# One decoder block on one core: the order of the attention steps on TensorE, the factor transposes and spread, and the pooling maps

## The chip, the cores and the metric

The kernel runs on one core of a Trainium2 chip. The metric is the device time of one execution in microseconds (us). A core has TensorE (PE in the profile; its weight loads are shown apart as PEld), VectorE (DVE), ScalarE (ACT), GpSimd (POOL), and SyncE (SP), which here only issues transfers. Each engine works through its own list of instructions in order and waits at semaphores for the others.

## The reference, cut to what matters

One layer, 512 tokens, width 1024: a SwiGLU layer, a token-mixing layer, a second SwiGLU layer, and a final norm, all modulated by a condition vector. The change lies in the token mixing:

```python
def token_mixing(u, cos, sin, w_in, w_pool, pool_scale, w_pool_branch, w_attn_branch, w_out):
    proj = u @ w_in
    p, q, k, v, gate_logits = jnp.split(proj, cuts, axis=-1)
    y_pool = multiscale_pool(p, w_pool, pool_scale)      # per group g: trailing mean minus token, times w_pool[g] (64x64), times scale
    q, k = rope(q), rope(k)
    for gi, (window, dilation) in enumerate(((128, 1), (512, 4), (2048, 16))):   # 4 heads of 64 each
        o, lse = dilated_window_attention(q[gi], k[gi], v[gi], window // dilation, dilation)
    wts = softmax(stack(lses))                           # over the three groups
    y_attn = sum_g wts[g] * outs[g]
    g_pool, g_attn = split(sigmoid(gate_logits))
    merged = g_pool * (y_pool @ w_pool_branch) + g_attn * (y_attn @ w_attn_branch)
    return merged @ w_out
```

## The kernel before, in words

Activations lie as channels by tokens: 128 channels on the partitions, 512 tokens along them, the tokens stored by residue class (c = token mod 4, then i = token div 4, "p (c i)"). All large products are made from two parts, high and low (`whi`, `wlo` of the weights, `UH`, `UL` of the activations): ScalarE writes the high part (line 377), VectorE subtracts to get the low part (line 389), and TensorE adds three products (lines 421 to 423 for 512 columns; 750 to 752 for 256 columns; 1779 to 1781 for the value tiles). The splits run a few tiles ahead of TensorE, in a ring. The order on every engine is the order in which the Python code issues the instructions; there is no scheduler.

The attention is cut into units (kind, n, hp): kind 0 is the undilated group (four blocks n of 128 queries), kind 1 are the two dilated groups together (four residue classes n = c); hp is a pair of heads. Each unit passes through five steps:

- `at_scores`: products of q and k, 64 rows deep (one head lies on 64 partitions), into `bS`; line 1470.
- `at_exp`: VectorE adds the mask and takes the maximum (1486, 1488), ScalarE the exponential (1491), which gives `prob`.
- `at_turn`: TensorE transposes `prob` in blocks of 128x128 into `bT` (1503), ScalarE copies to `probT` (1506, 1509).
- `at_values`: products of v (64 columns wide) and `probT` into `bO` (1521); for the second pair of heads VectorE copies `bO` out (1527 for kind 1, 1529 for kind 0).

These steps are strewn into the large products. `hooks` returns, for the sixth contraction step (k = 5) of a 512-column tile, a list of steps: the new units' scores, the transposes of the units whose scores were made one tile earlier, and the values of those of two tiles earlier. Eight projection tiles carry kind 0 (every second tile has new units, so transposes alternate with values and scores), the second pooling tile and the four value tiles (c = 0 to 3) carry kind 1. The last values of kind 1 are issued in the first gate product (`first`).

Then, inside the first group of gate products (`gate_duo`), `third` issues two things: `pool_map`, which multiplies the pooled differences `pd` (in `ev`, stored in token order "p (i c)") by the four 64x64 matrices of `wpool`, in four quarter tiles of the array (line 1622), and copies the two banks with the scale to a high part (ScalarE, 1626) and a low part (VectorE, 1627); and `at_fT`, which turns the eight softmax factors `f` of each 128-token block into eight rows over 512 tokens (line 1561), split into high rows 0 to 7 and low rows 32 to 39 of `fT` (1564, 1565). In the second group, `ends` calls `at_spread`: four products of `fT` with a 0/1 matrix `sel` (1571) that spread the factors to all channels, for `at_y` (1577 to 1579). `clear`, at the value tile c = 1, fills `fT` with zeros and writes `sel` (1760, 1761).

Of the kernel before, what the change touches and what calls it, by code (L numbers as in the profile page):

```python
# [9 lines left out]
F32R = mybir.dt.float32r  # L10
I32 = mybir.dt.int32
AF = mybir.ActivationFunctionType
OP = mybir.AluOpType

P = 128
T = 512
# [142 lines left out]
def chunk_widths():  # L159
    outs = [D] * (KT // 2 * (len(PARTS) - 1)) + [(FT - PARTS[-1][0]) * P] * KT  # L160
    f1 = [2 * FIRST * P] * KT + [D] * (2 * (FT - FIRST)), outs
    mix = [D] * 20 + [w for _, ms in GROUPS for w in [D] * 4 + [4 * P] * len(ms)] + [D] * KT
    return f1, mix, ([D] * (2 * FT), outs)


class Kernel:
# [5 lines left out]

    def plan(self):
        (i1, o1), mix, (i2, o2) = chunk_widths()
        self.chunks = []
        for name, ws in (("wf1i", i1), ("wf1o", o1), ("wmix", mix), ("wf2i", i2), ("wf2o", o2)):
            off, rec = 0, []
            for w in ws:
                rec.append((name, off, w))
                off += P * w  # L180
            self.chunks.append(rec)
# [1375 lines left out]
    def at_fT(self, bank):  # L1557

        nc, v = self.nc, self.nc.vector
        for n in range(4):  # L1560
            nc.tensor.matmul(bank[:8, n * P:n * P + P], self.f[:, n, :], self.ident, start=True, stop=True,
                             skip_group_check=True)
        by, b = (lambda x: x.rearrange("p (c n i) -> p n c i", c=4, n=4)), bank[:8].rearrange("p (n c i) -> p n c i", n=4, c=4)
        nc.scalar.activation(by(self.fT[:8]), b, AF.Copy)
        v.tensor_tensor(by(self.fT[32:40]), b, by(self.fT[:8]), op=OP.subtract)
# [48 lines left out]
    def pool_map(self, high, low):  # L1614

        nc = self.nc
        self.PH, self.PL = high, low
        banks = (self.bO, self.bS[0])
        for t in range(2):
            for r in range(2):  # L1620
                rows = slice(64 * r, 64 * r + 64)
                nc.tensor.matmul(banks[r][64 * t:64 * t + 64], self.wpool[rows, t * P + 64 * r:t * P + 64 * r + 64],
                                 self.pd[t][rows].rearrange("p (i c) -> p c i", c=4), start=True, stop=True, skip_group_check=True)
        for r, b in enumerate(banks):
            sc = self.vecs[:, 104 + r:105 + r]
            nc.scalar.activation(self.PH[r], b, AF.Copy, scale=sc)
            nc.vector.scalar_tensor_tensor(self.PL[r], b, sc, self.PH[r], op0=OP.mult, op1=OP.subtract)

    def mix(self):
        nc, tc = self.nc, self.tc  # L1630
# [8 lines left out]
        x = [xs[:, i * D:(i + 1) * D] for i in range(3)]  # L1639
# [4 lines left out]
        with tc.tile_pool(name="rt", bufs=1) as self.rt, tc.tile_pool(name="aw", bufs=2) as self.aw:  # L1644
# [5 lines left out]
            self.o23 = self.qt[0].rearrange("p (a t) -> p a t", a=2)  # L1650
            self.st, self.stn, self.f = (self.stp.tile([P, 4, 8], F32, name=x) for x in ("st", "stn", "f"))

            self.fT, self.sel = (self.stp.tile([64, T], F32R, name=x) for x in ("fT", "sel"))
            self.m1, self.l1 = (self.stp.tile([P, 16], F32, name=x) for x in ("m1", "l1"))
            masks = ma.tile([P, 4 * P], F32, name="masks")
            nc.sync.dma_start(masks, self.a["cst"][:, 163:675])
# [28 lines left out]
            for n in range(4):  # L1685
# [3 lines left out]
                b = self.nb()  # L1689
# [21 lines left out]

            def hooks(new, extra=(), between=()):
                sc, old = pipe
                todo = [(self.at_values, old), (self.at_turn, sc), (lambda f: f(), between), (self.at_scores, new),
                        (self.at_exp, new)]
                h = {5: [lambda f=f, u=u: f(u) for f, us in todo for u in us]}
                for k, f in extra:
                    h.setdefault(k, []).append(f)
                pipe[0], pipe[1] = list(new), sc
                return h  # L1720


            todo = [x for n in range(4) for x in ([(0, n, hp) for hp in range(2)], [])]
            rest = []
            for g in (1, 2):
                for dst in (self.qt[g], self.kt[g]):
                    for hp in range(2):
                        more = [((2, 7)[not hp], self.bg)] if dst is self.qt[1] else []
                        b = self.mm_tile(hooks(todo.pop(0), rest + more + [(7, self.bg)]))
                        rt = [self.scratch(2 * i + hp)[:, :T] for i in range(2)]  # L1730
                        self.rope_a(b, dst, hp, *rt)

                        rest = [(6, lambda dst=dst, hp=hp, w=rt[1]: self.rope_b(dst, hp, w))]


            g23 = [[(1, c, hp) for hp in range(2)] for c in range(4)]
            b = self.mm_tile(hooks([], rest + [(3, self.bg)]))
            self.pool_diff(0, b)
            assert self.ada_next == 59 and not self.adat, self.ada_next
# [11 lines left out]
            self.X, self.retired = [self.AR, self.cs], []  # L1751
            self.ready = True
            b = self.mm_tile(hooks(g23[0], [(3, u["copies"]), (4, u["adds"]), (7, self.bg)]))
            self.pool_diff(1, b)
            assert self.ada_next == 60 and not self.adat, self.ada_next
# [3 lines left out]
            def clear():  # L1759
                v.memset(self.fT.bitcast(F32), 0.0)  # L1760
                v.tensor_tensor(self.sel.rearrange("p (j d) -> p j d", j=8),
                                *(self.ident[:64, r:r + 8, None].to_broadcast([64, 8, 64]) for r in (0, 32)), op=OP.add)

            def free():
                self.held += 1
# [2 lines left out]

            held = self.held
            beside = [(1, 7, clear), (2, 2, lambda: u["whole"](0)), (2, 6, u["x0"]), (2, 6, u["x2"]), (2, 7, lambda: u["hi"](0)),  # L1770
                      (3, 0, u["x1"]), (3, 0, lambda: u["lo"](0)), (3, 2, self.at_swap), (3, 2, lambda: u["hi"](1)), (3, 3, free)]
            for c in range(4):
                hk = hooks(g23[c + 1] if c < 3 else [], [(k, f) for n, k, f in beside if n == c])
                b = self.nb()
# [436 lines left out]
```

## Time and profile before

| what | value |
|---|---|
| three runs | 966.43, 965.83, 966.37 us; median 966.37 |
| profiled execution: its own time | 965.6 us |
| its span (first to last instruction) | 963.7 us |
| granted TensorE clock | 0.999 |
| PE busy | 954.6 us (99%), 7278 matmuls |
| DVE, ACT, POOL busy | 839.2 us (87%), 539.4 us (56%), 88.5 us (9%) |

A busy time is the union of an engine's instructions. TensorE's instructions overlap in the pipeline (a 512-column product is shown as 0.39 us long, though the next one starts 0.23 us later), so the cost of a group on TensorE is read from start to start, not from its length. A plain fp32 product is shown as two records, a high and a low pass; the split products and the transposes as one.

### The profile page before, as it was taken

To read this page: it belongs to the slowest core of one execution; us is meant where nothing else is said; L and a number is where in the kernel's file an instruction comes from. 1 tells how busy PE (TensorE), PEld (TensorE's weight loads), DVE (VectorE), ACT (ScalarE), POOL (GpSimd) and SP (SyncE) were. 2 spreads that over 40 slices of the span, in tenths; PEclk is the share of its full clock that TensorE was granted. 3 is DMA by queue.
4 is the path that set the end of the run, shared out by engine and by line. 5 is a ranking of instruction groups with operands and counts; after the bars stand their busy time and mean duration, and the time that the engine had idled before them with its cause. 6 is when DMAs were issued, how large, how long until landed. Compare 5 with 4: busy or idle time off the path is not lost.

```text
span 963.7 us, 18130 instructions
## 1 busy us (share of the span) xinstructions
PE 954.6 (99%) x7278; PEld 897.1 (93%) x7278; DVE 839.2 (87%) x1237; ACT 539.4 (56%) x813; POOL 88.5 (9%) x106
## 2 busy tenths in 40 slices
PE   9999999999999999999999999999999999999997
PEld 7888999999999899878889998998999999999997
DVE  7989999899998779887897877989899888989886
ACT  5443666664755554444565453465665747566655
POOL 0000110101000003005410000000101100110002
PEclk9999999999999999999999999999999999999999
DMA  9857786786767648766356446724757666665632
GB/s 353 285 177 259 183 248 163 197 217 154 209 174 224 209 150 241 241 207 191 85 154 193 121 124 209 245 72 116 190 143 196 165 165 169 168 170 140 170 83 88
DMA packets 54087, 174.71 MB, mean 181 GB/s; under 512 B 7793, under 2 KB 10481, under 8 KB 53746
## 3 DMA queue, kind: packets, MB, share of 16 engines
q1 hardware_dynamic: 44416, 141.29, 44.6%
q0 software_dynamic: 9008, 31.72, 18.2%
q8 instruction: 57, 0.93, 0.4%
q10 hardware_dynamic: 578, 0.53, 0.2%
q14 instruction: 28, 0.23, 0.1%
HBM read 135.36 MB, written 2.24 MB: 143 GB/s over the span
## 4 chain that ended last, share of the span: by engine, by line
PE 92%; DVE 3%; DMA 2%; issue 1%; ACT 1%; POOL 0%; SPq 0%; POOLq 0%; DVEq 0%; ACTq 0%
PE bank L752 13%; PE bank L751 13%; PE bank L750 13%; PE bank L421 9%; PE bank L422 9%; PE bank L423 9%; PE bank L1111 4%; PE bank L1110 4%; PE bank L1109 4%; PE bank L2133 2%; PE bank L2135 2%; PE bank L2137 2%; DMA raw<-raw 1%; DVE wlo L389 1%; PE bank L1470 1%
## 5 line engine op out<-in xcount | busy, mean ns | idle before, releaser
L389 DVE TENSOR_TENSOR wlo<-raw,whi 128x1024 fp32r<-128x1024 f32 (+3 forms) x150 | 166.5, 1119 | 37.5 <-ACT whi L377 37.3
L750 PE MATMUL bank<-UH,whi 128*128 128x256 f32 x672 | 185.7, 276 | 0.0
L751 PE MATMUL bank<-UL,whi 128*128 128x256 f32 x672 | 185.6, 276 | 0.0
L752 PE MATMUL bank<-UH,wlo 128*128 128x256 f32 x672 | 185.6, 276 | 0.0
L389 DVE TENSOR_TENSOR wlo<-X,whi 128x1024 fp32r<-128x1024 f32 (+3 forms) x133 | 142.4, 1083 | 16.8 <-ACT whi L377 16.5
L377 ACT ACTIVATE whi<-raw 128x1024 fp32r<-128x1024 f32 (+3 forms) x150 | 142.6, 964 | 21.4 <-DMA raw<-wf1o 8.5
L377 ACT ACTIVATE whi<-X 128x1024 fp32r<-128x1024 f32 (+3 forms) x133 | 123.1, 946 | 52.8 <-DVE X L312 46.7
L750 PEld LDWEIGHTS bank<-UH,whi 128*128 128x128 f32 x672 | 126.1, 188 | 0.2
L751 PEld LDWEIGHTS bank<-UL,whi 128*128 128x128 f32 x672 | 126.3, 188 | 0.0
L752 PEld LDWEIGHTS bank<-UH,wlo 128*128 128x128 f32 x672 | 126.2, 188 | 0.0
L752 PE MATMUL bank<-SH,wlo 128*128 128x256 f32 x408 | 112.7, 276 | 0.3 <-DVE wlo L389 0.3
L750 PE MATMUL bank<-SH,whi 128*128 128x256 f32 x408 | 112.7, 276 | 0.0
L751 PE MATMUL bank<-SL,whi 128*128 128x256 f32 x408 | 112.6, 276 | 0.0
L421 PE MATMUL bank<-UH,whi 128*128 128x512 f32 (+1 forms) x272 | 92.8, 341 | 0.0
L422 PE MATMUL bank<-UL,whi 128*128 128x512 f32 (+1 forms) x272 | 91.9, 338 | 0.1
L423 PE MATMUL bank<-UH,wlo 128*128 128x512 f32 (+1 forms) x272 | 91.5, 337 | 0.0
L752 PEld LDWEIGHTS bank<-SH,wlo 128*128 128x128 f32 x408 | 76.6, 188 | 0.5 <-DVE wlo L389 0.5
L750 PEld LDWEIGHTS bank<-SH,whi 128*128 128x128 f32 x408 | 76.6, 188 | 0.1
L751 PEld LDWEIGHTS bank<-SL,whi 128*128 128x128 f32 x408 | 76.6, 188 | 0.0
L1109 PE MATMUL bank<-HI,whi 128*128 128x256 f32 x224 | 61.8, 276 | 0.0
L1110 PE MATMUL bank<-HK,whi 128*128 128x256 f32 x224 | 61.8, 276 | 0.0
L1111 PE MATMUL bank<-HI,wlo 128*128 128x256 f32 x224 | 61.8, 276 | 0.0
(408 smaller groups left out, 2404.3 us busy)
## 6 DMA issues: line engine op xcount, KB each, us to landing
raw<-wmix SPq DMA_DIRECT2D x44, 512.0 KB, 4.4
raw<-wf1i SPq DMA_DIRECT2D x32, 512.0 KB, 5.8
raw<-wf2i SPq DMA_DIRECT2D x30, 512.0 KB, 4.4
ada<-wada SPq DMA_DIRECT2D x23, 512.0 KB, 5.5
X<-raw POOLq DMA_DIRECT2D x23, 512.0 KB, 5.7
xs<-wada SPq DMA_DIRECT2D x17, 512.0 KB, 5.4
X<-wf2i SPq DMA_DIRECT2D x14, 512.0 KB, 4.5
X<-wf1i SPq DMA_DIRECT2D x11, 512.0 KB, 4.6
```

What stands on the lines that cost most here:

```text
L377: self.nc.scalar.activation(self.hi[:, y], r[:, x], AF.Copy)
L389: self.nc.vector.tensor_tensor(self.lo[:, y], r[:, x], self.hi[:, y], op=OP.subtract)
L421: M(ps, hi, uh, start=start, stop=False)
L422: M(ps, hi, ul, start=False, stop=False)
L423: M(ps, lo, uh, start=False, stop=stop)
L750: M(o, hi, uh, start=start and p == 0 and k == 0, stop=False, skip_group_check=True)
L751: M(o, hi, ul, start=False, stop=False, skip_group_check=True)
L752: M(o, lo, uh, start=False, stop=k == 3, skip_group_check=True)
L1109: M(o, hi, uh, start=start and m % 2 == 0 and k == 0, stop=False, skip_group_check=True)
L1110: M(o, hi, ul, start=False, stop=False, skip_group_check=True)
L1111: M(o, lo, uh, start=False, stop=k == 1, skip_group_check=True)
L2133: M(b, hi, self.UH[k], start=k == 0, stop=False)
```

## The change

Four edits:

1. In `hooks` the order of the steps at k = 5 becomes scores, values, transposes; it was values, transposes, scores. (`between` is never used.) The maximum and the exponential stay last.
2. `at_fT` uses the transpose operation in place of a product with the identity matrix.
3. `fT` and `sel` get 128 rows in place of 64 (the new ones hold zeros), so that the four spread products are 128 rows deep.
4. `pool_map` reads `pd` in the order in which it is stored; the result lies in the banks in token order, and the scaled copies of ScalarE and VectorE read the banks with a stride of four elements to write the residue-class order.

```diff
 def at_fT(self, bank):
-            nc.tensor.matmul(bank[:8, n * P:n * P + P], self.f[:, n, :], self.ident, start=True, stop=True,
-                             skip_group_check=True)
+            nc.tensor.transpose(bank[:8, n * P:n * P + P], self.f[:, n, :], self.ident)
...
 def pool_map(self, high, low):
-                                 self.pd[t][rows].rearrange("p (i c) -> p c i", c=4), start=True, stop=True, skip_group_check=True)
+                                 self.pd[t][rows], start=True, stop=True, skip_group_check=True)
         for r, b in enumerate(banks):
-            sc = self.vecs[:, 104 + r:105 + r]
-            nc.scalar.activation(self.PH[r], b, AF.Copy, scale=sc)
-            nc.vector.scalar_tensor_tensor(self.PL[r], b, sc, self.PH[r], op0=OP.mult, op1=OP.subtract)
+            sc, b = self.vecs[:, 104 + r:105 + r], b.rearrange("p (i c) -> p c i", c=4)
+            H, L = (x[r].rearrange("p (c i) -> p c i", c=4) for x in (self.PH, self.PL))
+            nc.scalar.activation(H, b, AF.Copy, scale=sc)
+            nc.vector.scalar_tensor_tensor(L, b, sc, H, op0=OP.mult, op1=OP.subtract)
...
-            self.fT, self.sel = (self.stp.tile([64, T], F32R, name=x) for x in ("fT", "sel"))
+            self.fT, self.sel = (self.stp.tile([P, T], F32R, name=x) for x in ("fT", "sel"))
...
             def hooks(new, extra=(), between=()):
-                todo = [(self.at_values, old), (self.at_turn, sc), (lambda f: f(), between), (self.at_scores, new),
+                todo = [(lambda f: f(), between), (self.at_scores, new), (self.at_values, old), (self.at_turn, sc),
                         (self.at_exp, new)]
...
             def clear():
-                                *(self.ident[:64, r:r + 8, None].to_broadcast([64, 8, 64]) for r in (0, 32)), op=OP.add)
+                                *(self.ident[:, r:r + 8, None].to_broadcast([P, 8, 64]) for r in (0, 32)), op=OP.add)
```

No instruction is added or taken away on any engine, and the lists of VectorE, ScalarE, GpSimd and SyncE keep their order; only TensorE's order changes, at six hooks. One of them is the hook of the value tile c = 1. On TensorE, between two products of that tile (lines 1781 and 1779; `bank_91` is its bank), there stood before:

```order
L1781 MATMUL bank_91<-whi,UL 128x512
L1521 MATMUL bank_97<-probT,v_3520 64x128 x8
L1503 MATMUL bank_90<-cst,prob 128x128 x4
L1503 MATMUL bank_92<-cst,prob 128x128 x4
L1470 MATMUL bank_93<-k_3517,q_3514 128x128
L1470 MATMUL bank_94<-k_3517,q_3514 128x128
L1470 MATMUL bank_93<-k_3518,q_3515 128x128
L1470 MATMUL bank_94<-k_3518,q_3515 128x128
```

and the last four rows once more, for the other pair of heads. Now, with the first four score rows above left out, there stand:

```order
L1470 MATMUL bank_93<-k_3517,q_3514 128x128
L1470 MATMUL bank_94<-k_3517,q_3514 128x128
L1470 MATMUL bank_93<-k_3518,q_3515 128x128
L1470 MATMUL bank_94<-k_3518,q_3515 128x128
L1521 MATMUL bank_97<-probT,v_3520 64x128 x8
L1503 MATMUL bank_90<-cst,prob 128x128 x4
L1503 MATMUL bank_92<-cst,prob 128x128 x4
L1779 MATMUL bank_91<-whi,UH 128x512
```

The scores moved from the end to the front, so the transposes (full tiles of the array) now stand next to the large products (full tiles too). At c = 2 it is the same; at c = 0 there are no values, and the transposes and the scores change places.

At three hooks of kind 0 there are values and scores and no transposes; the piece of the difference on TensorE at the second of them (bank_96 is the projection tile's bank):

```order
 L422 MATMUL bank_96<-UL,whi 128x512
 L423 MATMUL bank_96<-UH,wlo 128x512
-L1521 MATMUL bank_97<-probT,v_3519 64x128 x8
 L1470 MATMUL bank_93<-k_3516,q_3513 128x256
 L1470 MATMUL bank_94<-k_3516,q_3513 128x256
 L1470 MATMUL bank_93<-k_3516,q_3513 128x256
 L1470 MATMUL bank_94<-k_3516,q_3513 128x256
+L1521 MATMUL bank_97<-probT,v_3519 64x128 x8
 L421 MATMUL bank_96<-UH,whi 128x512
 L422 MATMUL bank_96<-UL,whi 128x512
```

Here the values moved behind the scores, and the number of neighbours of another kind stays the same.

## The prediction

> **What bounds the kernel now.** I read the page's busy times and its chain first, then the table of 20 us stretches, then TensorE's timeline at each place that the diff touches.
>
> ```profile
> PE 954.6 (99%) x7278; PEld 897.1 (93%) x7278; DVE 839.2 (87%) x1237; ACT 539.4 (56%) x813; POOL 88.5 (9%) x106
> PE 92%; DVE 3%; DMA 2%; issue 1%; ACT 1%; POOL 0%; SPq 0%; POOLq 0%; DVEq 0%; ACTq 0%
> 460.00:480.00 20.00, 20.00 (x149) 16.17 (x146) 16.82 (x35) 10.35 (x25) 8.98 (x7) 1.00 0.31 75
> ```
>
> TensorE is busy 99% of the span and carries 92% of the chain that ended last. In the stretch from 460 to 480 us it is busy all 20.00 us, at a granted clock of 1.00, while VectorE has 3.2 us free. So a microsecond taken from TensorE's list there is a microsecond of the program, as long as nothing that it waits for becomes late. The whole change is about TensorE's list, and the sum is made from start to start on it.
>
> **Part 1, the order of the steps.** TensorE pays when it passes from one shape of tile to another. The hook of the value tile c = 1, before:
>
> ```profile
> 458.96 0.39 PE L1781 MATMUL bank<-whi,UL 128*128 128x512 f32 x1
> 459.28 1.09 PE L1521 MATMUL bank<-probT,v 128*64 128x128 f32 x16
> 460.31 1.09 PE L1503 MATMUL bank<-cst,prob 128*128 128x128 f32 x8
> 461.33 1.16 PE L1470 MATMUL bank<-k,q 64*128 64x128 f32 x16
> 462.42 0.50 PE L1779 MATMUL bank<-whi,UH 128*128 128x512 f32 x1
> 462.76 0.40 PE L1780 MATMUL bank<-wlo,UH 128*128 128x512 f32 x1
> ```
>
> From the last product to the second one after the hook it takes 0.32 (into the values) + 1.03 (values) + 1.02 (transposes, then into the scores) + 1.09 (scores) + 0.34 = 3.80 us. How long the same stretches take beside other neighbours is shown at two other hooks. Transposes that are followed by a large product (c = 3):
>
> ```profile
> 478.04 1.10 PE L1503 MATMUL bank<-cst,prob 128*128 128x128 f32 x8
> 478.89 0.47 PE L1779 MATMUL bank<-whi,UH 128*128 128x512 f32 x1
> 479.20 0.40 PE L1780 MATMUL bank<-wlo,UH 128*128 128x512 f32 x1
> ```
>
> and scores that follow one and are followed by one:
>
> ```profile
> 383.68 0.39 PE L423 MATMUL bank<-UH,wlo 128*128 128x512 f32 x1
> 384.00 0.72 PE L1470 MATMUL bank<-k,q 64*128 64x128 f32 x8
> 384.64 0.50 PE L421 MATMUL bank<-UH,whi 128*128 128x512 f32 x1
> ```
>
> Eight transposes before a large product take 0.85 us, not 1.02; the step into scores costs 0.32, as that into values. The new order is 0.32 + 1.09 (scores) + 1.03 (values) + 0.85 (transposes) + 0.31 = 3.60 us: 0.20 saved, at c = 1 and at c = 2, 0.40 together. At c = 0 there are no values:
>
> ```profile
> 451.31 0.39 PE L1781 MATMUL bank<-whi,UL 128*128 128x512 f32 x1
> 451.54 1.04 PE L1503 MATMUL bank<-cst,prob 128*128 128x128 f32 x8
> 452.51 1.16 PE L1470 MATMUL bank<-k,q 64*128 64x128 f32 x16
> ```
>
> Before 0.23 + 0.97 + 1.09 + 0.34 (the last two as at c = 1) = 2.63; after 0.32 + 1.09 + 0.85 + 0.31 = 2.57; 0.06 saved. At the three hooks of kind 0 values and scores only change places. The values there, and the last ones of kind 1 before a large product:
>
> ```profile
> 409.94 1.09 PE L1521 MATMUL bank<-probT,v 128*64 128x128 f32 x16
> 410.97 1.14 PE L1470 MATMUL bank<-k,q 64*128 64x256 f32 x8
> ```
>
> ```profile
> 483.94 1.09 PE L1521 MATMUL bank<-probT,v 128*64 128x128 f32 x16
> 484.97 0.38 PE L427 MATMUL bank<-UH,whi 128*128 128x240 f32 x1
> ```
>
> Sixteen values take 1.03 us before scores and 1.03 before a large product, so nothing is won or lost there. What no row shows is the step from scores straight into values or transposes (six times now). I price it like the step from scores into a large product; the values before two different neighbours differ by 0.00, the transposes by 0.17, so between -0.05 and +0.05 at each is a fair bound: 0.3 us to either side. I take 0.46 us for part 1.
>
> Who waits differently: the copy of the values (1527, 1529) is ahead of the masked maximum in VectorE's queue, and the values come about 1.1 us later in the hook. At kind 0 VectorE reaches that copy late: in the hook above it starts at 412.86, and the values, which ended near 411.0, will end near 412.1. At c = 1 the new order is a gain:
>
> ```profile
> 412.86 0.42 DVE L1529 COPY o<-bank 128x256 f32<-128x256 f32 x1
> 462.52 0.42 DVE L1486 CUSTOM_DVE_ANT_0 prob<-bank,masks 128x256 f32<-128x256 f32 x1 [1.68 <-PE bank L1470]
> 476.18 0.69 DVE L1782 COPY v<-bank 128x512 f32<-128x512 f32 x1
> 477.01 1.09 PE L1521 MATMUL bank<-probT,v 128*64 128x128 f32 x16
> ```
>
> VectorE stood 1.68 us for the scores. Now they are there before the values, the copy runs when the values end near 461.4, and the maximum starts near 461.9, 0.6 us sooner. That matters, since VectorE then works without a wait up to the copy of `v` at 476.18, which ends (476.87) only 0.14 us before the values that read it. TensorE will be there 0.46 us sooner, VectorE 0.6: no stall.
>
> **Part 2, the factor transposes.** Parts 2 and 4 stand next to each other:
>
> ```profile
> 496.18 2.01 PE L1622 MATMUL bank<-ev,wpool 64*64 64x512 f32 x8
> 498.12 1.04 PE L1561 MATMUL bank<-cst,f 128*8 128x128 f32 x8
> 499.09 0.38 PE L427 MATMUL bank<-UH,whi 128*128 128x240 f32 x1
> ```
>
> The four products with the identity are eight records (two passes each) in 0.97 us. A transpose of `prob` is one record (eight of them in 0.85 us, 0.106 each), so four records go: 0.43 saved.
>
> The Trainium skill speaks against this term: TensorEngine Tiling (Array Packing), section Restrictions and Gotchas, says that column tiling excludes the transpose mode for fp32 input, and an output of eight rows is built into a tile of 32 columns. By that rule the two passes stay and the sum is smaller by 0.43; no row here has a transpose of so few columns.
>
> **Part 3, the spread.**
>
> ```profile
> 507.55 0.28 PE L751 MATMUL bank<-UL,whi 128*128 128x256 f32 x1
> 507.67 0.28 PE L752 MATMUL bank<-UH,wlo 128*128 128x256 f32 x1
> 507.88 1.20 PE L1571 MATMUL bank<-fT,sel 64*128 64x512 f32 x4
> 509.00 0.38 PE L427 MATMUL bank<-UH,whi 128*128 128x240 f32 x1
> 509.22 0.29 PE L750 MATMUL bank<-k,whi 128*128 128x256 f32 x1
> ```
>
> The step in costs 0.21 against 0.12 between equals, the four 512-column products 1.12 against 4 x 0.23 = 0.92 at the pace of the large ones (451.31 to 451.54), the step out 0.22 against about 0.12. At full depth all four are ordinary products: 0.09 + 0.20 + 0.10 = 0.39 saved, and never less than nothing, since the depth of a product does not lengthen it in these rows. The fill of `fT` and the write of `sel` on VectorE go over twice the partitions with as many elements on each; I cost them at nothing.
>
> **Part 4, the pooling maps.** The eight records (four quarter tiles at once, two passes) take 1.94 us, about 0.91 a pass, since the second four start at 497.1:
>
> ```profile
> L1622 PE MATMUL bank<-ev,wpool x8: 1074/1081/1092, 496.2 to 497.1; 64*64 64x512 f32 x8
> L1470 PE MATMUL bank<-k,q 64*128 64x256 f32 x24 | 3.4, 402 | 0.0
> ```
>
> For plain fp32 with operands in a row, eight score records of 128 columns take 0.64 us (384.00 to 384.64) and sixteen 1.09, so a pass of a pair costs 0.112 per 128 columns; 512 columns are 0.45. That is half of what the strided read takes. Bounds: nothing saved, if four streams at once are the limit, and 2 x (0.91 - 0.45) = 0.92. The values show two streams of 128 partitions at once, at (1.03 - 0.1) / 8 = 0.116 per pair and 128 columns; four streams of 64 partitions read as many rows, so I take the full 0.92.
>
> The Trainium skill has this in Advanced Engine Details and Errata, section Memory Cachelines: SBUF is read in lines of 16 bytes, and a read that finds each element in another line pays; four fp32 is just that stride. The length of 1081 ns agrees, and by that rule the 0.92 follows; without it the term would stay anywhere from 0 to 0.92.
>
> The stride now falls on two copies each of ScalarE and VectorE, out of the banks:
>
> ```profile
> L1626 ACT ACTIVATE xs<-bank,vecs 128x512 fp32r<-128x512 f32 x2 | 1.3, 686 | 0.0
> L1596 ACT ACTIVATE v<-bank 128x512 f32<-128x512 f32 x1 | 1.1, 1056 | 0.0
> 502.20 0.68 DVE L1565 TENSOR_TENSOR fT<-bank,fT 8x512 fp32r<-8x512 f32 x1
> ```
>
> A copy that writes with this stride takes 1056 ns, where one in a row takes 686; a strided read may cost nothing or as much. At the dear end ScalarE loses 2 x 0.4 and VectorE about as much. Behind them in the queues is `fT` (done at 502.88), which the spread reads at 507.88. That lead of 5.0 us shrinks by what TensorE saves before it (0.46 + 0.43 + 0.92 = 1.8) to 3.2, more than 1.6. So I cost it at nothing.
>
> **The sum.** 0.46 + 0.43 + 0.39 + 0.92 = 2.20 us less on TensorE. The profiled execution took 965.6 (span 963.7, 1.9 around it), so it would take 963.4; the median of the three runs is 0.8 above it, and on that median I predict 966.37 - 2.20 = 964.2. The later part follows, since ScalarE and VectorE there wait for TensorE again and again.
>
> **The rivals.** A measurement of this kernel tells 0.2% (1.93 us) from no change.
>
> - The pooling maps stay as long, because the four quarter tiles are the limit and not the stride. For it: no other row has four streams; against it: the two-stream pace. Gain 1.28, time 965.1. Chance 0.12.
> - The transposes of eight rows still take two passes. Gain 1.77, time 964.6. Chance 0.10.
> - A part of the gain turns into a wait: the copy of `v` with its 0.14 us of lead, if VectorE doesn't come sooner, holds TensorE by 0.46 - 0.14 = 0.32; with the unshown steps out of the scores dearer by 0.3 in all, the gain is about 1.6. Time 964.8. Against it: the 1.68 us that VectorE gets back. Chance 0.16.
> - Slower: the strided reads of the banks hold up `fT`. They decide once they add more than 3.2 us on ScalarE and VectorE in a row. At four times the length of 686 ns they add 2 x 2.06 = 4.1 on each, 8.2 together; the spread waits 5.0, less 2.2 won is 2.8 slower: 969.2. The nearest row shows 1.5 times, so chance 0.04.
> - The forecast: 964.2, chance 0.58, a little of which falls short of 0.2% since the sum is near that bound.
>
> **How the numbers follow.** Faster by over 0.2% (below 964.4): the forecast but for 0.04, and a step out of the scores that is cheaper than counted, 0.55 together. Within 0.2%: the first three rivals and that remainder, 0.41. Slower: 0.04. Low end: 0.3 more from the six unshown steps, 0.1 from a factor transpose that is a full tile and so saves its step out, and 0.4 for the spread of the runs: 963.4. High end: the pooling maps not shortened, and 0.2 lost beside it: 965.3. This leaves out the slow case and a few in a hundred at either end.
>
> **What would show it.** In the changed kernel's profile the hook at c = 1 should take 3.6 us from product to product, `prob` transposes should be followed by a large product 0.85 after their start, line 1561 should have four records, the pooling maps eight records of about 0.6 us within 1.0, the spread four records at a pace of 0.23 with no longer first one, and ScalarE's and VectorE's scaled copies their lengths under the stride. A wait of TensorE for the copy of `v` or for `fT`, eight records in line 1561, or pooling records still near 1.08 us would make the prediction wrong.

## The result and the profile after

The changed kernel took 963.2 us (median of 7, 962.49 to 964.25), the kernel before 966.37 on the same chip (median of 7, 965.83 to 968.3): ratio 0.9969, 95% interval 0.9959 to 0.9979. Measured again later, the ratio was 0.9966 (0.9954 to 0.9978). The kernel is faster. The forecast was 964.2 with a range of 963.4 to 965.3, so the sign was right and the time fell 0.2 us below the range: the gain was larger than the sum.

The busy times and the chain of the changed kernel's page (span 961.0 us, own time 962.81):

```profile
PE 952.0 (99%) x7274; PEld 896.5 (93%) x7274; DVE 838.4 (87%) x1237; ACT 539.1 (56%) x813; POOL 86.5 (9%) x106
PE 94%; DVE 2%; issue 1%; DMA 1%; ACT 1%; POOL 0%; POOLq 0%; ACTq 0%
```

TensorE is still the bound and has 2.6 us less of work, with four records fewer. The changed places follow in order of time. The hook of the value tile c = 1, TensorE's rows and then VectorE's:

```profile
458.41 0.39 PE L1781 MATMUL bank<-whi,UL 128*128 128x512 f32 x1
458.72 1.16 PE L1470 MATMUL bank<-k,q 64*128 64x128 f32 x16
459.82 1.09 PE L1521 MATMUL bank<-probT,v 128*64 128x128 f32 x16
460.84 1.09 PE L1503 MATMUL bank<-cst,prob 128*128 128x128 f32 x8
461.69 0.48 PE L1779 MATMUL bank<-whi,UH 128*128 128x512 f32 x1
462.01 0.40 PE L1780 MATMUL bank<-wlo,UH 128*128 128x512 f32 x1
```

```profile
460.96 0.43 DVE L1527 COPY q<-bank 128x256 f32<-128x256 f32 x1 [1.38 <-PE bank L1521]
461.54 0.42 DVE L1486 CUSTOM_DVE_ANT_0 prob<-bank,masks 128x256 f32<-128x256 f32 x1 [0.15 <-PE bank L1503]
474.94 0.68 DVE L1782 COPY v<-bank 128x512 f32<-128x512 f32 x1
```

From product to product it is 462.01 - 458.41 = 3.60 us, 0.20 less, as forecast; the transposes take 0.85 us up to the large product. VectorE reaches the maximum at 461.54 in place of 462.52 and the copy of `v` at 474.94 in place of 476.18; 0.48 of this the execution was ahead already at 446 us. The pooling maps and the factor transposes (L427 is an extra product of 240 columns that the kernel issues ahead of some gate products):

```profile
495.19 1.09 PE L1621 MATMUL bank<-ev,wpool 64*64 64x512 f32 x8
496.20 0.60 PE L1561 MATMUL bank<-cst,f 128*8 128x128 f32 x4
496.56 0.36 PE L427 MATMUL bank<-UH,whi 128*128 128x240 f32 x1
496.76 0.28 PE L750 MATMUL bank<-UH,whi 128*128 128x256 f32 x1
L1621 PE MATMUL bank<-ev,wpool x8: 589/614/640, 495.2 to 495.7; 64*64 64x512 f32 x8
```

Start to start, the pooling maps went from 1.94 to 1.01 us (records from 1081 to 614 ns), the factor transposes from 0.97 to 0.36, four records in place of eight. The strided copies out of the banks:

```profile
L1626 ACT ACTIVATE xs<-bank,vecs 128x512 fp32r<-128x512 f32 x2 | 1.3, 686 | 0.0
L1627 DVE SCALAR_TENSOR_TENSOR PL<-bank,vecs,xs 128x512 fp32r<-128x512 f32 x2 | 1.4, 744 | 0.0
```

ScalarE's take 686 ns as before, VectorE's 744 against 742: the stride costs nothing on this side. The spread:

```profile
504.83 0.28 PE L752 MATMUL bank<-UH,wlo 128*128 128x256 f32 x1
504.94 1.07 PE L1570 MATMUL bank<-fT,sel 128*128 128x512 f32 x4
505.85 0.27 PE L427 MATMUL bank<-UH,whi 128*128 128x240 f32 x1
505.96 0.28 PE L750 MATMUL bank<-k,whi 128*128 128x256 f32 x1
```

0.11 in, 0.91 for the four, 0.11 out, where it was 0.21, 1.12 and 0.22.

One thing had not been in any term. The gate products between the factor transposes and the spread were issued faster. Their groups in a stretch of 7 us, first before (500 to 507 us), then after (498 to 505); the last numbers are the busy time in us, the mean length of a record in ns, and the idle time ahead of them:

```profile
L751 PE MATMUL bank<-UL,whi 128*128 128x256 f32 x21 | 5.9, 281 | 0.0
...
L752 PE MATMUL bank<-UH,wlo 128*128 128x256 f32 x21 | 5.8, 276 | 0.0
```

281 ns go with one start every 117.8 ns, 276 with one every 113.3; no other values occur for long. The granted clock is 1.00 in both stretches. Some 65 of these products start 4.5 ns closer together, which is 0.28 us.

At 622 us a few tenths are given back. TensorE waits there for VectorE, which had itself waited for a load; the first row is that wait in the kernel before:

```profile
608.50 1.23 DVE L448 SCALAR_TENSOR_TENSOR v<-v,cond 128x1024 f32<-128x1024 f32 x1 [0.65 <-DMA v<-wada]
...
605.71 1.23 DVE L448 SCALAR_TENSOR_TENSOR v<-v,cond 128x1024 f32<-128x1024 f32 x1 [1.15 <-DMA v<-wada]
622.50 0.71 PE L509 MATMUL bank<-ones,AR 128*128 128x128 f32 x4 [0.21 <-DVE AR L624]
```

### The profile page after: what moved, and what is told of

It reads as the page before. It is cut to its first block, busy times and chain, and to the rows that moved or that the text cites. A ratio compares the mean times of both kernels' runs of the same rounds, so it can differ in the third digit from the quotient of the medians.

```text
span 961.0 us, 18119 instructions
## 1 busy us (share of the span) xinstructions
PE 952.0 (99%) x7274; PEld 896.5 (93%) x7274; DVE 838.4 (87%) x1237; ACT 539.1 (56%) x813; POOL 86.5 (9%) x106
## 4 chain that ended last, share of the span: by engine, by line
PE 94%; DVE 2%; issue 1%; DMA 1%; ACT 1%; POOL 0%; POOLq 0%; ACTq 0%
PE bank L750 14%; PE bank L752 14%; PE bank L751 14%; PE bank L421 8%; PE bank L422 8%; PE bank L423 8%; PE bank L1111 5%; PE bank L1109 5%; PE bank L1110 5%; PE bank L2133 2%; PE bank L2135 2%; PE bank L2137 2%; DMA v<-wada 1%; PE bank L1470 1%; PE bank L1521 1%
```

## How the runs are compared

Single executions of one kernel differ by a microsecond or more in places that the change doesn't touch. So each experiment is read locally: the ordinary products are the same in all kernels, and the start of each, less its start in the first profile of before, is a shift. The table (worked out from the traces, us, negative is earlier) gives by how much the shift changes in each stretch of before's time: 446 to 495 holds the steps of c = 0 to 3, 495 to 499.6 the pooling maps and factor transposes, 499.6 to 507.3 the gate products, 507.3 to 509.8 the spread, 509.8 to 560 what follows; "later" is 622 to 640, outside the sum.

```
kernel             446-495  495-499.6  499.6-507.3  507.3-509.8  509.8-560    sum   later
changed             -0.51     -1.55       -0.28        -0.44        0        -2.79   0.55
changed, again      -0.51     -1.55       -0.28        -0.44        0        -2.79   0.31
before, again        0.17      0           0            0           0         0.17  -0.01
order alone         -0.51      0           0            0           0        -0.51   0.39
transposes alone     0.01     -0.63        0           -0.01        0.62     -0.01   0.34
spread alone        -0.03      0           0           -0.40        0        -0.43   0.32
pool alone           0.01     -0.92       -0.29        -0.02        0        -1.21   0.28
changed, no settle  -0.51     -1.66       -0.29        -0.44        0        -2.90   1.33
changed, no settles -0.62     -1.66       -0.29        -0.56        0.62     -2.51   0.73
stride 2            -0.51     -1.50       -0.29        -0.44        0        -2.74   0.33
stride 8            -0.51     -0.60       -0.28        -0.44        0        -1.83   0.23
ft as 128x128       -0.51     -1.00        0           -0.42        0        -1.93   0.09
without pool        -0.51     -0.63        0           -0.41        0        -1.55   1.42
before, no settle    0.13     -0.11       -0.29        -0.02        0        -0.28   0.07
before, 224          0.16      0          -0.29        -0.02        0        -0.15   0.37
before, 256          0.18      0.01       -0.29        -0.02        0        -0.12   0.32
changed, 256        -0.51     -1.55       -0.29        -0.44        0        -2.79  -0.02
```

The changed kernel's stretch of 2.79 us comes back within 0.01 us in its second execution. All later readings use this table and the rows shown with them.

## The four parts, each alone

**The order** (line 1714 of before, nothing else):

```
-  todo = [(self.at_values, old), (self.at_turn, sc), (lambda f: f(), between), (self.at_scores, new),
+  todo = [(lambda f: f(), between), (self.at_scores, new), (self.at_values, old), (self.at_turn, sc),
```

> The kernel before, with the new order of an attention step alone (hooks and scores, then values, then transposes); transposes, spread and pooling maps as before. Theory A, that each part has its own price on TensorE and the prices add: the ordinary products of the changed kernel draw ahead of before's by 0.51 us between 446 and 484 us (0.06 in c=0, 0.20 in c=1, 0.20 in c=2, 0.03 in c=3), so here too 0.45 to 0.55 us, and nothing at the kind-0 steps; the pooling map stays at eight records of 1.08 us, the factor transposes at 0.97 us, the spread at 0.43 us more than after. Time 0.5 us under before if the loss near 625 us does not come, 0.0 to 0.2 if it does. Rival B, that the gain comes from the shorter wait of VectorE's maximum alone and is lost at the next wait on VectorE: the shift is back to under 0.2 us by 484.

965.91 us against 966.59, ratio 0.9994 (0.9984 to 1.0003): not told from before as a whole. Locally 0.51 us, at the same four places as in the changed kernel (0.08, 0.20, 0.20, 0.03), and nothing at the hooks of kind 0. Rival B falls: nothing is lost up to 560 us.

**The factor transposes** (line 1561):

```
-  nc.tensor.matmul(bank[:8, n * P:n * P + P], self.f[:, n, :], self.ident, start=True, stop=True, ...)
+  nc.tensor.transpose(bank[:8, n * P:n * P + P], self.f[:, n, :], self.ident)
```

> The kernel before, with the factor transposes as transposes (one pass) alone. Theory A: L1561 shows 4 records in place of 8 and the stretch from its start to the settling product's start goes from 0.97 to 0.36 us (0.61). Theory P1, that the pace of the gate products behind it (113.3 ns each after, 117.8 ns before, from 497 to 505 us) hangs on what ran on TensorE right before them: the fast pace shows here as well, 0.27 us more, 0.9 us in all. Rival P2, that the pace hangs on the pooling map or on the other engines: the pace here stays 117.8 ns and the gain stops at 0.61 us.

967.02 us, ratio 1.0007 (0.9994 to 1.002): no gain to be seen. The trace tells why. TensorE's rows at the transposes, and the gate products' group from 512 to 526 us:

```profile
500.37 0.60 PE L1561 MATMUL bank<-cst,f 128*8 128x128 f32 x4
500.73 0.36 PE L427 MATMUL bank<-UH,whi 128*128 128x240 f32 x1
500.92 0.28 PE L750 MATMUL bank<-UH,whi 128*128 128x256 f32 x1
...
L750 PE MATMUL bank<-UH,whi 128*128 128x256 f32 x19 | 5.3, 281 | 0.0
```

The 0.61 of theory A is there, but the slow pace goes on behind the spread, for 144 more products up to 528 us, and takes 0.62 back. In before it had ended at the spread. P1 in the form expected (the transposes themselves set the pace) falls. P2 had the pace right as far as the spread, but not the gain, which it saw stop at 0.61.

**The spread** (lines 1653 and 1762, `fT` and `sel` on 128 rows):

```
-  self.fT, self.sel = (self.stp.tile([64, T], F32R, name=x) for x in ("fT", "sel"))
+  self.fT, self.sel = (self.stp.tile([P, T], F32R, name=x) for x in ("fT", "sel"))
...
-  *(self.ident[:64, r:r + 8, None].to_broadcast([64, 8, 64]) for r in (0, 32)), op=OP.add)
+  *(self.ident[:, r:r + 8, None].to_broadcast([P, 8, 64]) for r in (0, 32)), op=OP.add)
```

> The kernel before, with the spread on 128 rows alone. Theory A: the stretch from L1570's start to the next gate product goes down by 0.45 us (what the shift shows at 506 us of the changed kernel) and nothing else moves; VectorE's two preparations on 128 rows stay at 0.48 and 0.63 us, off the path. Rival, that the wait moves to the copies of the spread maps: TensorE gains under 0.2 us at 506. Time 0.2 to 0.5 us under before, at the bound of what can be told.

966.03 us, ratio 0.9995 (0.9985 to 1.0005); locally 0.40, near the 0.45 of theory A; the rival falls. Twice the rows cost VectorE nothing that counts: in the changed kernel its two preparations take 0.49 and 0.63 us, in before 0.49 and 0.62. This execution also shows a part of what makes the runs differ: in the attention steps near 404 us, ahead of all that was changed here, TensorE waited for the probabilities, and the shift grew by 1.9 us.

```profile
PE bank L1503 <- ACT prob L1491: 0.9, 1, 0.9
```

The row counts the wait ahead of the eight transposes; the rest lies among them, since they took 1.67 us from start to start, 0.81 in the first profile of before. Growth there was 1.5 us in the profiles of the order and the transposes alone, 0.8 in the second of before, 0 in the first of before, in the changed kernel and in the pooling maps alone. It occurs with and without each part.

**The pooling maps** (lines 1622 to 1628):

```
-  self.pd[t][rows].rearrange("p (i c) -> p c i", c=4), start=True, ...
+  self.pd[t][rows], start=True, ...
...
-  nc.scalar.activation(self.PH[r], b, AF.Copy, scale=sc)
+  sc, b = ..., b.rearrange("p (i c) -> p c i", c=4)
+  H, L = (x[r].rearrange("p (c i) -> p c i", c=4) for x in (self.PH, self.PL))
+  nc.scalar.activation(H, b, AF.Copy, scale=sc)
```

> The kernel before, with the pooling maps in token order and the strided reads at the copies alone. Theory A: eight records of 0.61 us in place of 1.08, 0.93 us less from the pooling map's start to the factor transposes' start, copies at 0.69 and 0.74 us as before. Theory P1 (pace from what runs right before the gate products): they stay at 117.8 ns, so 0.93 in all; rival P2 (pace from the pooling map or from the time at which the other engines work): 113.3 ns here too, 1.2 us in all. Time 0.9 to 1.2 us under before, 0.4 to 0.6 less if the loss near 625 us follows from TensorE's being early.

964.83 us, ratio 0.9985 (0.9976 to 0.9995), the only part whose gain is seen in the whole time. TensorE's rows, and the gate products' group from 499.5 to 506 us:

```profile
495.99 1.09 PE L1622 MATMUL bank<-ev,wpool 64*64 64x512 f32 x8
497.00 1.04 PE L1561 MATMUL bank<-cst,f 128*8 128x128 f32 x8
497.98 0.38 PE L427 MATMUL bank<-UH,whi 128*128 128x240 f32 x1
...
L750 PE MATMUL bank<-UH,whi 128*128 128x256 f32 x20 | 5.5, 276 | 0.0
```

0.92 from the maps and 0.29 from the pace, 1.21 in all, as rival P2 had it. The parts alone, the transposes read before their loss, give 0.51 + 0.63 + 0.40 + 1.21 = 2.75; together they gave 2.79. Apart from the pace, they add; the pace doesn't, since it took 0.62 from the transposes alone and nothing from all four together.

## Both kernels once more, and the stride

The kernel before, unchanged:

> The kernel before once more, to see what one profiled execution can differ by from another of the same kernel. Theory N, that the upstream differences (1.5 to 2.0 us lost between 391 and 404 us in three of the four single-part kernels, and the 0.3 to 0.55 us lost at 626 us in the changed kernel and in all four) are loads that land late in some executions: here the shift against the first profile of before moves by some tenths to 2 us at 306, 400 or 626 us, and by nothing between 446 and 520 us. Rival S, that the loss at 626 follows from TensorE's being early there: no loss at 626 here. The ratio is 1 within 0.0010.

965.97 us against 966.85 for its other runs on that chip, ratio 0.9993 (0.9984 to 1.0002). The shift moved by 0.8 us at 404, so theory N holds for that place. At 626 it lost nothing here. Over all rows of the table the loss there is between 0 and 1.42 us. With the order of before it reaches 0.37 us at most. The four losses above 0.5 all belong to kernels with the new order, but six others with the new order lost 0.39 or less, and the changed kernel with another extra product lost nothing. It is not a fixed price of being early (rival S). It goes with VectorE's waits for two loads: in the two profiles that lost 1.33 and 1.42 us they were 1.00 and 1.26, and 1.08 and 1.44; in the first of before 0.42 and 0.65. Why the loads land as they do, and whether being early makes a large loss more likely, was not tested.

The expectation that nothing moves from 446 to 520 was wrong by 0.17 us: such a loss, 0.13 to 0.18, stands in four of the seven other profiles with the old order, at the values of c = 3. There, in one of them (before with 256 columns, below), the copy of `v` ends at 476.44 and the values start 0.14 later:

```profile
475.76 0.68 DVE L1782 COPY v<-bank 128x512 f32<-128x512 f32 x1
476.08 0.39 PE L1781 MATMUL bank<-whi,UL 128*128 128x512 f32 x1
476.58 1.09 PE L1521 MATMUL bank<-probT,v 128*64 128x128 f32 x16
```

From the last product to the values it is 0.50 us here, 0.35 in the first profile of before, where the values also start 0.14 after the copy, and 0.32 in the changed kernel. So the 0.14 us that the prediction read as a lead is the time that the release takes: there was no lead, and TensorE waited 0.03 us even in that profile. That is the 0.03 which the new order gains at c = 3. No profile with the new order has that wait. In the changed kernel the copy of `v` ends at 475.62 and the values start at 476.02, so that a lead of 0.26 us beyond the 0.14 has come.

The changed kernel once more:

> The changed kernel once more, with more runs. If the single parts add (order 0.51, factor transposes 0.63, spread 0.40, pooling maps 0.92, and 0.1 to 0.3 of pace), the time is 2.5 to 2.8 us under before, ratio 0.9971 to 0.9974; the theory that the first measurement caught the changed kernel in quiet executions gives 2.2 us or less (ratio 0.9977 or above). Local readings in the trace: 2.2 to 2.3 us between 446 and 520 us as in the first profile if the pace of the gate products is 113.3 ns again, 0.27 us less if it is 117.8 here.

963.11 us against 966.85, ratio 0.9966 (0.9954 to 0.9978), on the side of the parts that add, though the interval just reaches the other theory's 0.9977. Locally it is 2.79 us, as in the first profile of the changed kernel; the expectation had misread that one as 2.2 to 2.3. Of the medians' 3.2 and 3.7 us the table explains 2.79, and 0.1 on average for the wait for `v`, less a few tenths at 626. The rest lies within the intervals (2.0 to 4.0 and 2.1 to 4.4 us), and what it is made of stays open.

Stride two at the pooling maps (the changed kernel with the operand read two elements apart, copies to match):

```
-  self.pd[t][rows], start=True, ...
+  self.pd[t][rows].rearrange("p (j a) -> p a j", a=2), start=True, ...
```

> The changed kernel with the pooling maps' moving operand read at a stride of two 4-byte elements instead of one, the copies reordered to match. Theory L, that a read costs by the 16-byte lines that a group of elements touches (1081 ns per record at stride four, 614 at stride one): at stride two half a line is used for each element pair, so something between, 770 to 900 ns. Theory W, that the array reads by pairs of elements and a stride up to two is free: 614 ns. Theory X, that any stride other than one is the slow way: 1081 ns.

And stride eight:

```
-  self.pd[t][rows], start=True, ...
+  self.pd[t][rows].rearrange("p (j k) -> p k j", k=8), start=True, ...
```

> The changed kernel with the pooling maps' moving operand read at a stride of eight 4-byte elements, copies reordered to match. Stride one took 614 ns a record, two 633, four 1081. Theory L, that an element alone on a 16-byte stretch is the whole price: 1081 ns again. Theory W, that the price goes with the bytes spanned: about 2000 ns. For the pace: the gate products behind ran at 117.8 ns in every kernel with the stride of four and at 113.3 in every one with a stride of one or two; if the slow pooling map sets it, 117.8 here, though the copies are those of the changed kernel; if the copies' order sets it, 113.3.

Their records, stride two and then eight:

```profile
L1621 PE MATMUL bank<-ev,wpool x8: 606/633/662, 497.3 to 497.9; 64*64 64x512 f32 x8
...
L1621 PE MATMUL bank<-ev,wpool x8: 1093/1099/1106, 495.2 to 496.1; 64*64 64x512 f32 x8
```

614, 633, 1081 and 1099 ns at strides one, two, four and eight: a step between two and four and no slope to either side. Theory W was right at two and wrong at eight, L the other way round. The rule in the Trainium skill, Advanced Engine Details and Errata, section Memory Cachelines, fits all four: it says that at least two hits on a 16-byte line are needed to absorb the access latency, and that another line for each access pays. It gives no size; the 0.92 us of the prediction came from the rows of the scores. The rival that four streams are the limit falls, since four streams run at 614 ns. The gate products behind the stride of eight ran at 113.3 ns, so slow pooling maps alone don't set the pace. Single executions took 964.75 (stride two) and 963.39 us (stride eight); they say nothing of a difference of 1 us.

## Which tile pays the step

The four factor transposes as ordinary products of a full tile (the identity on both sides, so this kernel leaves the factors out):

```
-  nc.tensor.transpose(bank[:8, n * P:n * P + P], self.f[:, n, :], self.ident)
+  nc.tensor.matmul(bank[:, n * P:n * P + P], self.ident, self.ident, start=True, stop=True, ...)
```

> The changed kernel with the four factor transposes replaced by four ordinary f32 products of a 128x128 tile (the identity on both sides, so the factors are left out of the result). It tells apart whether the 0.20 us that the transposes gave beyond the four records less comes from the tile or from the pass. Theory tile: a 128x8 tile costs a step out, a full tile does not: eight records of 109 ns, 0.87 us, and the next product starts at that pace (0.11 us after the last record's start, not 0.20). Theory pass: the 0.20 us belong to f32 products of two passes whatever their tile: the last record's start is 0.20 us ahead of the next product here as well, 0.97 us in all; then a transpose of 8 rows is as free of a step as one of 128.

```profile
498.80 1.16 PE L1561 MATMUL bank<-cst 128*128 128x128 f32 x8
499.71 0.36 PE L427 MATMUL bank<-UH,whi 128*128 128x240 f32 x1
499.91 0.28 PE L750 MATMUL bank<-UH,whi 128*128 128x256 f32 x1
...
L751 PE MATMUL bank<-UL,whi 128*128 128x256 f32 x21 | 5.9, 281 | 0.0
```

0.91 us for the eight records and 0.20 for the extra product. In the trace the last record starts 0.03 ahead of the extra product, where the 128x8 products had 0.20: the step out is gone, so the narrow tile of the products paid it. A step in of 0.10 has come instead, from the 64x64 tiles ahead (first record to second 0.21, the others 0.11). The transposes of eight rows pay neither: the steps between their starts are 0.11, 0.11, 0.11 and 0.03. The expectation of 0.87 left out the step in. The last row shows the slow pace, behind a pooling map without a stride.

Everything but the pooling maps together:

```
-  self.pd[t][rows], start=True, ...
+  self.pd[t][rows].rearrange("p (i c) -> p c i", c=4), start=True, ...      (and its copies as before)
```

> The changed kernel with the pooling maps and their copies as before: order, factor transposes and spread alone together. If the parts add, the stretch from 446 to 520 us is 0.51 + 0.63 + 0.42 = 1.56 us shorter than before as long as the pace behind the transposes equals before's (117.8 ns for some 70 products), and up to 0.6 us less than that if the slow pace lasts to 528 us as it did with the transposes alone; 1.87 us if the pace is 113.3 at once, which would clear the pooling map of it.

1.55 us less, against 1.56 expected, with the slow pace up to the spread; 966.08 us in one execution.

## What sets the pace

The extra product of 240 columns (L427, from `settle`) stands ahead of the sixth gate product. The changed kernel without it:

```
-  {1: None, 5: self.bT[0]})
+  {1: None})
```

> The changed kernel without the one extra 240-column product (L427) between the factor transposes and the sixth gate product. Theory P1, that this product sets the phase at which the gate products run on: without it the pace behind the transposes is 117.8 ns for some 70 to 140 products, a loss of 0.3 to 0.6 us against the 0.2 us that the product itself costs; the transposes' step-out shows between the last L1561 and the first L750. Rival P2, that it sets nothing any more behind full-tile transposes: pace 113.3 ns at once, 0.15 to 0.20 us faster than the changed kernel.

```profile
498.64 0.60 PE L1561 MATMUL bank<-cst,f 128*8 128x128 f32 x4
499.00 0.37 PE L750 MATMUL bank<-UH,whi 128*128 128x256 f32 x1
499.20 0.28 PE L751 MATMUL bank<-UL,whi 128*128 128x256 f32 x1
```

Locally 0.11 us better still, at the fast pace: P1 falls for this kernel, and P2's 0.15 to 0.20 us were too much. In whole time it was 964.22 us, ratio 0.9973 (0.9964 to 0.9981), which overlaps the changed kernel's: its profiled execution lost 1.33 us at 626 us. It is the best by its own stretch, but not shown faster than the changed kernel.

Without all three extra products of the stage:

```
-  {1: None, 5: self.bT[0]})
+  {})
...
-  self.gate_duo(*sc, p5, lambda n=1: None, beside, {1: None})
+  self.gate_duo(*sc, p5, lambda n=1: None, beside, {})
```

> The changed kernel without its three extra 240-column products in this stage: ahead of the second and the sixth gate product, and behind the spread. Measured so far: leaving out the one ahead of the sixth takes 0.11 us off the stretch from 446 to 520 us (2.90 us less than before in place of 2.79) at an unchanged pace of 113.3 ns. If the steps out of the other two are as cheap behind full tiles, another 0.1 us each, 3.1 us in all against before. The rival, that they do set the pace: the products behind the left-out one run at 117.8 ns, 0.3 us lost for 70 of them. The whole time can hardly tell either from the changed kernel: 962.9 to 963.3 us.

964.02 us, ratio 0.9974 (0.9962 to 0.9987). Two more products saved 0.22, and behind the spread 144 products ran slow (506.5 to 523.4 us), which cost 0.62: 2.51 us locally in place of the 3.1 expected. The rival was right there. One of their groups, 507 to 521 us:

```profile
L752 PE MATMUL bank<-k,wlo 128*128 128x256 f32 x16 | 4.5, 281 | 0.0
```

By now the slow pace had stood behind pooling maps with a stride and without, behind transposes and products, and the fast one too. What all slow cases at this place had was the 240 columns. So the kernel before was run with that product left out, at 224 and at 256 columns, and the changed one at 256:

```
-  self.settle(other if other is not None else bank, w[0][0], self.UH[0])
+  self.settle(other if other is not None else bank, w[0][0], self.UH[0], HT - SHIFT if other is None else 224)
```

> The kernel before without the extra 240-column product ahead of the sixth gate product. Theory start, that the first few products behind a restart fix the pace until the next interruption: the pace from 500 to 508 us may flip from 117.8 to 113.3 ns, 0.3 us less for 70 products, beside about 0.1 us for the product left out. Theory state, that the kernel before runs slow there whatever leads in: 117.8 ns as in its two profiled executions.

> The kernel before with that extra product at 224 columns in place of 240. Theory start: another width moves the start by some 7 ns and may flip the pace to 113.3 ns; theory state: 117.8 ns.

> The kernel before with that extra product at 256 columns in place of 240. Theory start: the pace may flip to 113.3 ns, in this one or in the one of 224 columns; theory state: 117.8 ns in both.

> The changed kernel with that extra product at 256 columns in place of 240. Theory start: the pace, 113.3 ns in three profiled executions with 240 columns or none, may flip to 117.8; theory state: 113.3 ns.

The groups of 7 us in the kernel before (no extra product, 224, 256 columns; starts at 500, 501 and 500 us):

```profile
L751 PE MATMUL bank<-UL,whi 128*128 128x256 f32 x22 | 6.1, 276 | 0.0
...
L751 PE MATMUL bank<-UL,whi 128*128 128x256 f32 x21 | 5.8, 276 | 0.0
...
L752 PE MATMUL bank<-UH,wlo 128*128 128x256 f32 x22 | 6.1, 276 | 0.0
```

All three flip to the fast pace and gain 0.29 us; theory state falls. In the changed kernel 256 columns changed nothing (-0.29 against -0.28). Each of these kernels was profiled once, so chance is a rival. It is there elsewhere: the run of some 70 products behind a wait at 305 us, ahead of all that was changed, was slow in three of the eighteen profiles (the transposes alone, no extra product, stride two) and fast in the others. Here are its products between 306.3 and 313.5 us, before and in the transposes alone:

```profile
L750 PE MATMUL bank<-UH,whi 128*128 128x256 f32 x16 | 4.4, 276 | 0.0
...
L750 PE MATMUL bank<-UH,whi 128*128 128x256 f32 x16 | 4.5, 281 | 0.0
```

At 500 us TensorE doesn't wait, and all four profiles with the lead-in of before (before twice, the order alone, the spread alone) ran slow, so chance is an unlikely account of three flips out of three. The likely reading is that the pace hangs on how the run of products starts, and that the kernel before had at this place a start that gave the slow one. Which start gives which is not settled: 240 columns gave the slow pace in before, behind the transposes alone and behind full-tile products, the fast one in the changed kernel and with the pooling maps alone. The four variants took 965.72, 967.25, 965.25 and 965.33 us, with shifts at 446 us from -0.6 to +2.6 us: single times tell nothing here.

## Why the prediction fell short

The four mechanisms that the sum priced were right. Two steps failed: the factor transposes were priced too low, and the pace of the gate products was put at nothing. By the table the sum of 2.20 should have been 2.79.

- **Part 1, the order: 0.46 forecast, 0.51 measured.** c = 1 and c = 2 came to 0.20 each, as worked out; c = 0 to 0.08 in place of 0.06, and 0.03 came at c = 3, the wait for `v` that went. The unshown steps out of the scores cost what the step into a large product does. VectorE reached the maximum 0.50 us sooner (0.98 less the 0.48 from upstream), where 0.6 was forecast.
- **Part 2, the factor transposes: 0.43 forecast, 0.62 measured. This step failed.** The sum priced the four records and kept the step out for eight rows; a saving there was put at 0.1 and only in the low end. The last record started 0.20 us ahead of the next product before, and 0.03 now: the step out was the narrow product's and went with it. The rule of the Trainium skill (TensorEngine Tiling (Array Packing), section Restrictions and Gotchas) that would have kept two passes, as the prediction applied it to eight rows, is not borne out: line 1561 has four records.
- **Part 3, the spread: 0.39 forecast, 0.44 measured** (0.40 alone).
- **Part 4, the pooling maps: 0.92 forecast, 0.92 measured**, with copies of 686 and 744 ns, so the slower rival had no place. `fT` was waited for in no run.
- **The pace: not in the sum, 0.28 measured. This step failed too.** The prediction took the cost of a gate product as the same in both kernels and looked only for waits; the products went from 117.8 to 113.3 ns. The rows of before held a sign of it, since 281 and 276 ns stood in groups of the same product. That the changed kernel got the fast pace here could not have been worked out from them, as far as is known.
- **The turn into a wait:** none at the copy of `v`; what was read as 0.14 us of lead there was no lead, and the new order took an occasional wait away.

With those terms the median of before gives 966.37 - 2.79 = 963.6, which lies inside the stated range; the low end, made the same way, would have held 963.2. The last 0.4 us between 963.6 and 963.2 is within the interval of the measurement (2.0 to 4.0 us of gain), and its cause stays open. The profiled execution that the sum stood on had also been a good one of before: no wait at 404 us and only 0.03 us at the copy of `v`.

## What to carry to other kernels

When TensorE is the bound, price a change of tile by both steps, in and out, from rows where the neighbours are the same; a transpose of a few rows can be free of both where the product of the same shape is not. Put the stride where reads are cheap: out of the accumulator banks it cost nothing here, into TensorE 1.8 times from a stride of four on. Measure gains under 0.2% locally, by the shift of unchanged instructions, since the whole time moves by a microsecond from one execution to the next for reasons elsewhere.

## What was new of the hardware

Identical products in one kernel run at one of two paces, 113.3 or 117.8 ns for 256 columns, at a granted clock of 1.00 in both. Behind the first few products of a run the pace is held until the stream is interrupted, over some 70 to 144 products in the slow runs told of here, 0.3 to 0.6 us each time. In the kernel before, another width of one product ahead of the run, or its absence, went with the fast pace, in one execution each; in the changed kernel it made no difference. The slow pace took back the whole gain of the transposes alone. Which start gives which pace stays open.
